# Gated linear attention: exponentials written in their layout of use, score copies and square sums on ScalarE

## The chip, the cores and the metric

The kernel runs on one core of one Trainium2 chip. The metric is the time of one execution on the device in microseconds (us); each kernel is run several times and the median counts. The engines are called PE (TensorE, matmuls), DVE (VectorE), ACT (ScalarE), POOL (GpSimd) and SP (SyncE, which here issues the loads and stores).

## The reference

The program is one layer of a bidirectional encoder for two sequences (called samples 0 and 1) of 512 tokens with 1024 features: a SwiGLU block, a mixing block, a second SwiGLU block and a gated input embedding. The mixing block has attention heads and four heads of gated linear attention (GLA) side by side. The change touches GLA alone. Per head (64 features of q and k, 128 of v) and per chunk of 64 tokens the reference computes

```python
cum = jnp.cumsum(log_a.reshape(bsz, nc, c, h, dk), axis=2)
mid = cum[:, :, c // 2 - 1:c // 2]
last = cum[:, :, c - 1:]
scores = jnp.einsum('bnihd,bnjhd->bnhij', q * jnp.exp(cum - mid), k * jnp.exp(mid - cum))
scores = jnp.where(mask, scores, 0.0)
o_intra = jnp.einsum('bnhij,bnjhe->bnihe', scores, v)
upd = jnp.einsum('bnjhd,bnjhe->bnhde', k * jnp.exp(last - cum), v)
...
o_inter = jnp.einsum('bnihd,bnhde->bnihe', q * jnp.exp(cum), states)
```

once forward (a token sees itself) and once backward (it does not). `states` is the running sum of `upd`, decayed from chunk to chunk. The two directions are added, each head's 128 values are divided by their root mean square, and the result is multiplied with a gate.

## The kernel before

The program has four stages: the first SwiGLU block, the mixing block, the second SwiGLU block and the end. PE's order is written out by hand: generators yield after each small piece of work, and a main generator of large matmuls is woven with a side generator by counts (the table PLAN). For DVE, ACT, POOL and SP a scheduler orders the instructions that the code issues, and each engine then works through its own list strictly in that order. Buffers come from pools: a pool of four PSUM banks (`bank_d`, named pd in the profile) serves all matmuls of GLA, another (pm) the large ones. `m8` is a pool of three large SBUF buffers, which take in turn the decays, the exponentials E, the decayed q and k (z, whose tile is named qk1; the profile calls it qk) and the states W; `m2` is one of six smaller buffers. A tile that takes over a buffer waits until the last reader of the old content is done.

GLA runs at the end of the mixing block, woven with the output projection's matmuls (L716, three per yield, in two or more yields between the pieces). Heads go in pairs; there are two pairs per sample, so four pairs, called first to fourth. `gla(s)` yields four generators for a sample:

- `pre(hp)` prepares a pair. Loads on SP bring the log decays l (L985, 4 issues) and q and k (L987, 2 issues) into one tile lq, with the two heads one above the other in the 128 partitions, 64 each. Four groups of matmuls (L999, two directions by two halves of the tokens) make the sums of the decays. Behind each, ACT writes exp(+) and exp(-) into E (the helper's line, L177), and DVE copies small columns sc (L1003), which become ex (L1010, L1012) and, through ACT, the chunk decays R. L1017 multiplies q and k with E into z: in z a head has 128 partitions, the forward direction in the lower 64 and the backward one in the upper 64, so each piece is a 64-partition product that moves from one half to the other; eight of them per pair.
- `one(h)` does a head: transposes of k (L1031) into a bank, copied by ACT to kT (L1033); the update matmuls (L1038) into two banks U; the chain of states: two copies by ACT (L1045, L1046), then six steps per direction on DVE (L1048, L1050), each reading a part of U and the state before it; POOL then scales all states with R (L1051, L1052). Score matmuls (L1060) fill two banks, S[0] forward and S[1] backward, and L1062 copies from each the entries under a mask into A, on DVE.
- `two_a(h)` makes the head's output in a bank: A times v (L1071) plus q times W (L1074). L1077 squares it on ACT into osq, L1079 sums the squares on DVE, the rms steps follow, and L1082 multiplies bank, rms and gate into G.
- `two_b(h)` transposes G (L1089) and splits it into a high and a low part (L1090 ACT, L1091 DVE) for the output projection.

Per pair PE does `one` for the even and the odd head, `two_a` for both, then `pre` of the next pair with its four groups, then `two_b` for both. Weights are loaded (raw), and split into a high part by ACT (L138) and a low part by POOL or DVE (L139).

Of the kernel before, what the change touches and what calls it, by code (L numbers as in the profile page):

```python
# [12 lines left out]
AF = mybir.ActivationFunctionType  # L13
ALU = mybir.AluOpType
AX = mybir.AxisListType
# [5 lines left out]
NT = 4  # L21
# [14 lines left out]
            A=(157, 159, 160),  # L36
            seg=((2, 132), (2, 142), (18, 160), (18, 170), (43, 193), (43, 216), (178, 334)),
            b=(4, 3),
# [685 lines left out]
class Middle:  # L724
# [246 lines left out]
    def gla(self, s):  # L971
        nc, L = self.nc, self.L
        f, bw = slice(0, 64), slice(64, 128)
        T = {}

        def pre(hp):
            if hp == 0:
                T["mx"] = L.xp.tile([128, 4, 2, 512], F32R, tag="x", name="mixG")
                self.mix[s, 0] = T["mx"]
                T["A"] = self.vp.tile([128, 2, NT, 128], F32, tag="v", name="A")  # L980
                nc.gpsimd.memset(T["A"], 0.0)
            lq = self.m8("lq", (128, 2, 2, 512))
            l, qk = lq[:, 0].rearrange("p d (t c) -> p d t c", t=NT), lq[:, 1]
            for t in range(NT):
                nc.sync.dma_start(l[:, :, t], self.spill["l", s][t].rearrange("p (d c) -> p d c", d=2)[:, :, hp * 128:(hp + 1) * 128])  # L985
            for i in range(2):
                nc.sync.dma_start(qk[:, i], self.spill["gqk", s][2 * i + hp])  # L987
            yield
            R = [self.sp.tile([128, 8], F32, tag=f"R{e}", name=f"R{e}", bufs=2) for e in range(2)]
            E = self.m8("E", (128, 2, 2, 512))  # L990
            z = self.m8("qk1", (128, 2, 2, 512))
            for e in range(2):
                T["z", 2 * hp + e], T["R", 2 * hp + e] = z[:, e], R[e]
            for dr in range(2):
                sc = self.sp.tile([128, 2, 8], F32, tag="sc", name="sc")
                for hf in range(2):
                    b = L.bank_d().rearrange("p (a n) -> p a n", a=2)
                    for a in range(2):
                        nc.tensor.matmul(b[:, a, :132], l[:, dr, 2 * hf + a], self.L.U[:, dr], start=True, stop=True)  # L999
                    for j, sg in ((0, 1.0), (1, -1.0)):  # L1000
                        L.expln(E[:, dr, j, hf * 256:(hf + 1) * 256].rearrange("p (a n) -> p a n", a=2),
                                             b[:, :, :128], AF.Exp, scale=sg)
                    nc.vector.tensor_copy(  # L1003
                        sc[:, :, hf * 4:hf * 4 + 4].rearrange("p k (a c) -> p a k c", a=2),
                        b[:, :, 128:132].rearrange("p a (k c) -> p a k c", k=2))
                    if hf == 0:
                        yield
                ex = self.sp.tile([128, 7], F32, tag="ex", name="ex")
                if dr == 0:
                    nc.vector.tensor_tensor(ex, sc[:, 1, 0:7], sc[:, 0, 1:8], ALU.add)  # L1010
                else:
                    nc.vector.tensor_tensor(ex, sc[:, 1, 1:8], sc[:, 0, 0:7], ALU.add)  # L1012
                for e in range(2):
                    rs, rd = slice(64 * e, 64 * e + 64), slice(64 * dr, 64 * dr + 64)
                    L.expln(R[e][rd, 1 - dr:8 - dr], ex[rs], AF.Exp)
                    for i in range(2):
                        nc.vector.tensor_tensor(z[rd, e, i], qk[rs, i], E[rs, dr, i], ALU.mult)  # L1017
                yield

        def one(h):  # L1020
# [8 lines left out]
            b = L.bank_d()  # L1029
# [26 lines left out]
            for t in range(NT):  # L1056
                ts = slice(t * 128, (t + 1) * 128)
                for dr in range(2):
                    rd = slice(64 * dr, 64 * dr + 64)
                    nc.tensor.matmul(S[dr][:, t], k1[rd, ts], q1[rd, ts], start=True, stop=True)  # L1060
            for dr in range(2):
                nc.vector.copy_predicated(A, self.L.mask[:, dr].unsqueeze(1).to_broadcast([128, NT, 128]), S[dr])  # L1062
            T["h", h] = gv, G, W, A
            yield

        def two_a(h):
            gv, G, W, A = T["h", h]
            q1 = T["z", h][:, 0]
            o = L.bank_d().rearrange("p (a n) -> p a n", a=4)
            for t in range(NT):  # L1070
                nc.tensor.matmul(o[:, t], A[:, t], gv[:, t], start=True, stop=False)  # L1071
                for cc in range(2):
                    c = 2 * t + cc
                    nc.tensor.matmul(o[64 * cc:64 * cc + 64, t], q1[:, c * 64:(c + 1) * 64], W[:, c],  # L1074
                                     start=False, stop=True)
            sq = self.m2("osq", shape=(128, NT, 128))
            nc.scalar.activation(sq, o, AF.Square)  # L1077
            ss = L.small(NT, "oss")
            nc.vector.tensor_reduce(ss, sq, AX.X, ALU.add)  # L1079
            r = self.rms(ss, NT, 128.0, GN_EPS, "gn")  # L1080
            for t in range(NT):
                nc.vector.scalar_tensor_tensor(G[:, t], o[:, t], r[:, t:t + 1], G[:, t], ALU.mult, ALU.mult)  # L1082
            yield
# [365 lines left out]
```

## Time and profile before

| what | value |
|---|---|
| time, median of 3 runs | 1935.41 us (1934.36 to 1936.28) |
| the profiled execution: its time | 1935.19 us |
| the profiled execution: its span | 1933.4 us |
| mean granted clock of PE | 0.992 |
| PE busy | 1867.3 us, 97% of the span |
| DVE busy | 1406.2 us, 73% |
| ACT busy | 874.0 us, 45% |
| POOL busy | 822.3 us, 43% |

The span runs from the first to the last instruction. An engine's busy time counts its instructions alone. In a row of a timeline stand start, duration, engine, line, operation, what is written and read, the shapes and the count, and in brackets the idle time before it with the instruction that ended the idle time. GLA lies between about 985 and 1130 us of the span.

### The profile page before, as it was taken

How to read it: one execution, taken by the hardware profiler on the slowest of the kernel's cores; microseconds unless marked ns; L12 is line 12 of the kernel's file. 1: busy time of each engine (PE TensorE's matmuls, PEld its weight loads, DVE VectorE, ACT ScalarE, POOL GpSimd, SP SyncE). 2: the span in 40 equal slices, each digit the busy share in tenths (PEclk: the TensorE clock that was granted, in tenths of full speed). 3: DMA queues.
4: the chain of work that ended last, by engine and by line, in shares of the span. 5: the costliest groups of instructions: out<-in, count | busy, mean ns of one | idle time of the engine just before them, and what ended most of it. 6: DMA issues, size and time to landing. Idle time of an engine off the chain costs nothing. (4 is left out here: it accounts for less than half of the span.)

```text
span 1933.4 us, 25273 instructions
## 1 busy us (share of the span) xinstructions
PE 1867.3 (97%) x8838; PEld 1529.5 (79%) x8838; DVE 1406.2 (73%) x2173; ACT 874.0 (45%) x1654; POOL 822.3 (43%) x614
## 2 busy tenths in 40 slices
PE   7999999999999998989999898999999999999999
PEld 5788888888888887777876577888888888888787
DVE  7856566657786985788778878656566568995973
ACT  6444544544231355657743356445444442231442
POOL 0665566552450023432234444654665561451243
PEclk9999999999999999999999998999999999999999
DMA  4434443468876233222443332335444388766242
GB/s 181 152 115 153 174 158 142 166 261 336 307 271 231 75 133 123 77 87 91 144 148 88 99 109 89 141 114 185 159 153 153 142 308 335 300 247 235 77 131 77
DMA packets 104959, 322.22 MB, mean 167 GB/s; under 512 B 11008, under 2 KB 38400, under 8 KB 99456
## 3 DMA queue, kind: packets, MB, share of 16 engines
q1 hardware_dynamic: 101376, 314.32, 45.3%
q10 hardware_dynamic: 3456, 6.29, 0.9%
q8 instruction: 70, 1.15, 0.3%
q14 instruction: 57, 0.47, 0.1%
HBM read 218.85 MB, written 101.71 MB: 166 GB/s over the span
## 5 line engine op out<-in xcount | busy, mean ns | idle before, releaser
L139 POOL TENSOR_TENSOR w<-raw,w 128x512 fp32r<-128x512 f32 (+1 forms) x288 | 391.5, 1367 | 651.6 <-ACT w L138 602.0
L138 ACT ACTIVATE w<-raw 128x512 fp32r<-128x512 f32 (+1 forms) x586 | 363.0, 624 | 435.2 <-POOL raw L270 85.2
L270 POOL TENSOR_TENSOR raw<-raw 128x512 f32<-128x512 f32 x240 | 356.8, 1494 | 226.2 <-DVE w L139 159.0
L426 PE MATMUL pm<-X,w 128*128 128x512 f32 x1848 | 435.2, 393 | 10.5 <-ACT X L138 7.4
L426 PEld LDWEIGHTS pm<-X,w 128*128 128x128 f32 x1848 | 348.1, 189 | 89.0 <-ACT X L138 8.2
L139 DVE TENSOR_TENSOR w<-raw,w 128x512 fp32r<-128x512 f32 (+1 forms) x298 | 281.9, 954 | 117.2 <-ACT w L138 113.2
L426 PE MATMUL pd<-X,w 128*128 128x512 f32 x1320 | 309.2, 392 | 2.9 <-DVE w L139 2.2
L426 PEld LDWEIGHTS pd<-X,w 128*128 128x128 f32 x1320 | 248.6, 189 | 57.9 <-DVE w L139 3.0
L540 PE MATMUL pm<-w,XB 128*128 128x512 f32 x864 | 198.4, 390 | 0.8 <-DVE Y L524 0.8
L540 PEld LDWEIGHTS pm<-w,XB 128*128 128x128 f32 x864 | 162.0, 188 | 35.2 <-DVE Y L524 1.6
L139 DVE TENSOR_TENSOR hs<-sg,hs 128x512 fp32r<-128x512 f32 (+1 forms) x182 | 145.2, 817 | 49.5 <-ACT hs L138 48.4
L716 PE MATMUL pm<-w,h1T 128*128 128x512 f32 (+1 forms) x768 | 180.2, 377 | 0.0
L138 ACT ACTIVATE hs<-sg 128x512 fp32r<-128x512 f32 (+1 forms) x182 | 98.4, 561 | 165.1 <-DVE sg L392 64.3
L716 PEld LDWEIGHTS pm<-w,h1T 128*128 128x128 f32 x768 | 133.1, 191 | 20.7
L540 PE MATMUL pd<-w,XB 128*128 128x512 f32 x648 | 148.8, 389 | 0.0
L540 PEld LDWEIGHTS pd<-w,XB 128*128 128x128 f32 x648 | 121.7, 188 | 25.2
L524 DVE TENSOR_TENSOR Y<-Y,pm 128x512 f32<-128x512 f32 x104 | 70.5, 683 | 35.4 <-PE pm L540 35.4
L372 DVE TENSOR_TENSOR sg<-u,pm 128x512 f32<-128x512 f32 x22 | 15.1, 687 | 108.9 <-PE pm L426 108.9
L716 PE MATMUL pm<-w,h3T 128*128 128x512 f32 x384 | 90.6, 393 | 0.0
L716 PEld LDWEIGHTS pm<-w,h3T 128*128 128x128 f32 x384 | 71.3, 188 | 14.7 <-DVE h3T L671 0.2
L661 ACT ACTIVATE pd<-pd,c_lnT 128x512 f32<-128x512 f32 x48 | 36.0, 751 | 92.8 <-PE pd L659 92.8
L524 DVE TENSOR_TENSOR Y<-Y,pd 128x512 f32<-128x512 f32 x88 | 58.7, 679 | 17.6 <-PE pd L540 17.6
(237 smaller groups left out, 2512.8 us busy)
## 6 DMA issues: line engine op xcount, KB each, us to landing
hs<-hs SPq DMA_DIRECT2D x126, 512.0 KB, 2.6
XB<-hs SPq DMA_DIRECT2D x42, 1536.0 KB, 6.8
raw<-in_wgu SPq DMA_DIRECT2D x88, 512.0 KB, 3.4
raw<-in_wd SPq DMA_DIRECT2D x36, 512.0 KB, 7.1
hs_t<-hs SPq DMA_DIRECT2D x56, 256.0 KB, 2.4
XB<-hs_t SPq DMA_DIRECT2D x26, 512.0 KB, 4.9
raw<-in_wout SPq DMA_DIRECT2D x16, 512.0 KB, 3.6
raw<-in_wpg SPq DMA_DIRECT2D x16, 512.0 KB, 3.6
```

The costliest lines, as they stand in the source:

```text
L138: first = nc.scalar.activation(hi, raw, AF.Copy)
L139: (eng or nc.vector).tensor_tensor(lo, raw, hi.bitcast(F32), ALU.subtract)
L270: (sums or self.nc.gpsimd).tensor_tensor(o(), x(), y(), ALU.subtract)
L372: add = lambda o, x, y: nc.vector.tensor_tensor(o, x, y, ALU.add)
L426: nc.tensor.matmul(bank, w[:, a, kt * 128:(kt + 1) * 128], X[k][:, kt, b], start=(k in (0, 1, 4) and kt == 0 and m == 0), stop=(kt == 3 an ...
L524: nc.vector.tensor_tensor(yv, yv, bank, ALU.add)
L540: nc.tensor.matmul(b[t], h[:, a, t * 128:(t + 1) * 128], d[:, c], start=(k in (0, 4, 1) and g == 0 and x == 0), stop=(g == len(H) - 1 and ...
L661: nc.scalar.activation(p, p, AF.Identity, scale=self.lnT[:, c:c + 1], bias=self.lnT[:, c + 8:c + 9])
L716: nc.tensor.matmul(banks[t][:, :width], x[:, i, t * 128:(t + 1) * 128], w[a][:, j], start=(q == 0 and a == 0 and m == 0), stop=(q == nq - ...
```

## The change

All line numbers of the kernel after are one to three higher than before in this stretch. The change has four parts.

1. l gets an m8 tile of its own. q and k are loaded straight into z, twice, once into the lower and once into the upper 64 partitions (L992, four issues instead of two).
2. E is written in z's layout: each exponential of 128x256 becomes two of 64x256, one per head, which write to the direction's 64 partitions. One in-place multiplication of 128x1024 per head (L1019), behind the second direction, takes the place of four of 64x512.
3. ACT copies the diagonal 64x64 blocks of S[1] to A (L1064, two copies of 64x4x64 per head); one predicated copy (L1065) then writes the forward entries from S[0] over them.
4. The square on ACT is made per token tile with an accumulated sum (L1082, four instructions of 128x128), and the reduction on DVE goes.

```diff
@@ -979,16 +979,17 @@
                 self.mix[s, 0] = T["mx"]
                 T["A"] = self.vp.tile([128, 2, NT, 128], F32, tag="v", name="A")
                 nc.gpsimd.memset(T["A"], 0.0)
-            lq = self.m8("lq", (128, 2, 2, 512))
-            l, qk = lq[:, 0].rearrange("p d (t c) -> p d t c", t=NT), lq[:, 1]
+            l = self.m8("l", (128, 2, 2, 512))[:, 0].rearrange("p d (t c) -> p d t c", t=NT)
             for t in range(NT):
                 nc.sync.dma_start(l[:, :, t], self.spill["l", s][t].rearrange("p (d c) -> p d c", d=2)[:, :, hp * 128:(hp + 1) * 128])
-            for i in range(2):
-                nc.sync.dma_start(qk[:, i], self.spill["gqk", s][2 * i + hp])
             yield
             R = [self.sp.tile([128, 8], F32, tag=f"R{e}", name=f"R{e}", bufs=2) for e in range(2)]
             E = self.m8("E", (128, 2, 2, 512))
             z = self.m8("qk1", (128, 2, 2, 512))
+            for i in range(2):
+                src = self.spill["gqk", s][2 * i + hp].rearrange("(e p) c -> p e c", e=2)
+                for rd in (f, bw):
+                    nc.sync.dma_start(z[rd, :, i], src)
             for e in range(2):
                 T["z", 2 * hp + e], T["R", 2 * hp + e] = z[:, e], R[e]
             for dr in range(2):
@@ -997,9 +998,10 @@
                     b = L.bank_d().rearrange("p (a n) -> p a n", a=2)
                     for a in range(2):
                         nc.tensor.matmul(b[:, a, :132], l[:, dr, 2 * hf + a], self.L.U[:, dr], start=True, stop=True)
-                    for j, sg in ((0, 1.0), (1, -1.0)):
-                        L.expln(E[:, dr, j, hf * 256:(hf + 1) * 256].rearrange("p (a n) -> p a n", a=2),
-                                             b[:, :, :128], AF.Exp, scale=sg)
+                    for e in range(2):
+                        for j, sg in ((0, 1.0), (1, -1.0)):
+                            L.expln(E[64 * dr:64 * dr + 64, e, j, hf * 256:(hf + 1) * 256].rearrange("p (a n) -> p a n", a=2),
+                                    b[64 * e:64 * e + 64, :, :128], AF.Exp, scale=sg)
                     nc.vector.tensor_copy(
                         sc[:, :, hf * 4:hf * 4 + 4].rearrange("p k (a c) -> p a k c", a=2),
                         b[:, :, 128:132].rearrange("p a (k c) -> p a k c", k=2))
@@ -1013,8 +1015,8 @@
                 for e in range(2):
                     rs, rd = slice(64 * e, 64 * e + 64), slice(64 * dr, 64 * dr + 64)
                     L.expln(R[e][rd, 1 - dr:8 - dr], ex[rs], AF.Exp)
-                    for i in range(2):
-                        nc.vector.tensor_tensor(z[rd, e, i], qk[rs, i], E[rs, dr, i], ALU.mult)
+                    if dr == 1:
+                        nc.vector.tensor_tensor(z[:, e], z[:, e], E[:, e], ALU.mult)
                 yield
 
         def one(h):
@@ -1058,8 +1060,9 @@
                 for dr in range(2):
                     rd = slice(64 * dr, 64 * dr + 64)
                     nc.tensor.matmul(S[dr][:, t], k1[rd, ts], q1[rd, ts], start=True, stop=True)
-            for dr in range(2):
-                nc.vector.copy_predicated(A, self.L.mask[:, dr].unsqueeze(1).to_broadcast([128, NT, 128]), S[dr])
+            for r in (f, bw):
+                nc.scalar.activation(A[r, :, r], S[1][r, :, r], AF.Copy)
+            nc.vector.copy_predicated(A, self.L.mask[:, 0].unsqueeze(1).to_broadcast([128, NT, 128]), S[0])
             T["h", h] = gv, G, W, A
             yield
 
@@ -1074,9 +1077,9 @@
                     nc.tensor.matmul(o[64 * cc:64 * cc + 64, t], q1[:, c * 64:(c + 1) * 64], W[:, c],
                                      start=False, stop=True)
             sq = self.m2("osq", shape=(128, NT, 128))
-            nc.scalar.activation(sq, o, AF.Square)
             ss = L.small(NT, "oss")
-            nc.vector.tensor_reduce(ss, sq, AX.X, ALU.add)
+            for t in range(NT):
+                nc.scalar.activation(sq[:, t], o[:, t], AF.Square, accum_out=ss[:, t:t + 1])
             r = self.rms(ss, NT, 128.0, GN_EPS, "gn")
             for t in range(NT):
                 nc.vector.scalar_tensor_tensor(G[:, t], o[:, t], r[:, t:t + 1], G[:, t], ALU.mult, ALU.mult)
```

The change also moves instructions. First PE, in the third pair, from the end of the even head's scores over the odd head's transposes to its update matmuls (pd and a number is one PSUM bank's tile, qk1 is z, w and mixA belong to the output projection; the brackets name the engines or load queues whose semaphores are waited for). Before:

```order
L1060 MATMUL pd_9481<-qk1_9333 128x128
L716 MATMUL pm_9271<-w_9103,mixA_6014 128x512 x3
L1031 MATMUL pd_9505<-c_ident_3477,qk1_9333 128x128 [waits DVE_49,Activation_49]
L1031 MATMUL pd_9505<-c_ident_3477,qk1_9333 128x128 x3
L716 MATMUL pm_9271<-w_9106,mixA_6014 128x512 x3
L1038 MATMUL pd_9516<-gvh_9495,kT_9510 128x128 [waits DMAHW4_49,DVE_49,Activation_49]
L1038 MATMUL pd_9517<-gvh_9495,kT_9510 128x128 [waits PE_49]
```

and of the kernel after:

```order
L1062 MATMUL pd_9505<-qk1_9351 128x128
L716 MATMUL pm_9289<-w_9117,mixA_6014 128x512 x3
L1033 MATMUL pd_9530<-c_ident_3477,qk1_9351 128x128 [waits PE_49,Activation_49]
L1033 MATMUL pd_9530<-c_ident_3477,qk1_9351 128x128 x3
L716 MATMUL pm_9289<-w_9120,mixA_6014 128x512 x3
L1040 MATMUL pd_9541<-gvh_9520,kT_9535 128x128 [waits DMAHW0_49,DVE_49,Activation_49]
L1040 MATMUL pd_9542<-gvh_9520,kT_9535 128x128 [waits DVE_49]
```

The sequence is the same, but the odd head's transposes no longer wait for DVE: their bank is now one that ACT and PE release. Both update banks now wait for DVE.

Next PE at the even head's output in the same pair, behind the odd head's scores. Before:

```order
L1060 MATMUL pd_9560<-qk1_9333 128x128
L716 MATMUL pm_9544<-w_9275,mixG_8603 128x512
L716 MATMUL pm_9544<-w_9275,mixG_8603 128x512 [waits Pool_49]
L716 MATMUL pm_9544<-w_9275,mixG_8603 128x512
L716 MATMUL pm_9545<-w_9272,mixG_8603 128x512 x3
L1071 MATMUL pd_9577<-gvh_9423,A_9318 128x128 [waits DVE_49,Activation_49]
L1074 MATMUL pd_9577<-W_9454,qk1_9333 64x128 [waits Pool_49]
```

and of the kernel after:

```order
L1062 MATMUL pd_9585<-qk1_9351 128x128
L716 MATMUL pm_9569<-w_9293,mixG_8603 128x512
L716 MATMUL pm_9569<-w_9293,mixG_8603 128x512 [waits Pool_49]
L716 MATMUL pm_9569<-w_9293,mixG_8603 128x512
L716 MATMUL pm_9570<-w_9290,mixG_8603 128x512 x3
L1074 MATMUL pd_9603<-gvh_9447,A_9338 128x128 [waits PE_49,Activation_49]
L1077 MATMUL pd_9603<-W_9478,qk1_9351 64x128 [waits Pool_49]
```

The first output matmul waits for PE and ACT instead of DVE and ACT; the wait for POOL, which scales W, is as before.

Then ACT between the odd head's output of the second pair and kT of the third pair's two heads (osq: squares; gna, gny: rms steps; E, R: exponentials). Before:

```order
L177 ACTIVATE R_9331<-ex 64x7
L177 ACTIVATE E<-pd 128x256 x2
L138 ACTIVATE w<-raw 128x512
L1090 ACTIVATE mixG<-pd,c_gn 128x512
L177 ACTIVATE R_9330<-ex 64x7
L177 ACTIVATE R_9331<-ex 64x7
L1090 ACTIVATE mixG<-pd,c_gn 128x512
L1033 ACTIVATE kT<-pd 128x512
L1045 ACTIVATE W<-pd 64x128
L1046 ACTIVATE W<-pd 64x128
L138 ACTIVATE w<-raw 128x512
L1033 ACTIVATE kT<-pd 128x512
```

and of the kernel after:

```order
L177 ACTIVATE E<-pd 64x256 x6
L138 ACTIVATE w<-raw 128x512
L177 ACTIVATE R_9348<-ex 64x7
L177 ACTIVATE R_9349<-ex 64x7
L138 ACTIVATE w<-raw 128x512
L1093 ACTIVATE mixG<-pd,c_gn 128x512 x2
L1035 ACTIVATE kT<-pd 128x512
L1047 ACTIVATE W<-pd 64x128
L1048 ACTIVATE W<-pd 64x128
L1064 ACTIVATE A<-pd 64x4x64 x2
L138 ACTIVATE w<-raw 128x512
L1035 ACTIVATE kT<-pd 128x512
```

The weight splits (L138) of this stretch stand behind all exponentials now, the second R pair is ahead of both mixG, and the even head's two copies to A, like the split behind them, stand between its W copies and the odd head's kT.

On SP the four loads of q and k for the second to fourth pair now wait for PE (the last reader of the buffer that z takes over), stand behind a weight load, and have the next pair's v and gate loads behind them; before, the two loads followed those of l and waited for a queue slot alone.

## The prediction

> **What bounds the kernel now.** I read the page first, then PE's waits over the stretch that the diff touches, then each engine's timeline there.
>
> ```profile
> PE 1867.3 (97%) x8838; PEld 1529.5 (79%) x8838; DVE 1406.2 (73%) x2173; ACT 874.0 (45%) x1654; POOL 822.3 (43%) x614
> ```
>
> TensorE (PE) is busy for 1867.3 of 1933.4 us, and the change takes no matmul away. What can be won is PE's idle time, and only where the gated linear attention (GLA) runs, about 985 to 1130 us. PE's waits there, with total, count and longest:
>
> ```profile
> PE pd L1031 <- DVE W L1048: 7.5, 4, 3.1
> PE pd L1031 <- DVE qk L1017: 5.5, 4, 1.8
> PE pd L1071 <- DVE W L1048: 5.0, 4, 1.3
> PE pd L1089 <- DVE Gh L1082: 0.8, 1, 0.8
> ```
>
> There are four head pairs, and each has three waits, all on VectorE (DVE): before the even head's transposes for the decayed q and k (5.5 us in all), before the odd head's transposes (7.5) and before the even head's output (5.0) for the state chain. The sum with the last line, 18.8 us, is the ceiling of any gain from waits. The busy time per stretch (PE, PEld, DVE, ACT, POOL, then PE's granted clock) shows who is full:
>
> ```profile
> 1100.00:1110.00 10.00, 6.81 (x54) 5.10 (x55) 9.60 (x21) 2.50 (x6) 4.17 (x7) 1.00 0.22 65
> 1110.00:1120.00 10.00, 8.94 (x62) 6.17 (x60) 7.68 (x18) 1.05 (x3) 4.66 (x4) 0.83 0.01 2
> ```
>
> Where PE drops to 6.81 of 10 us, DVE has 9.60 and ScalarE (ACT) 2.50. In the next stretch PE's clock is 0.83. So work moved from DVE to ACT can pay here. How much is seen in one head pair, the third, on PE (start, duration, idle before):
>
> ```profile
> 1066.06 0.63 PE L1031 MATMUL pd<-c_ident,qk 128*128 128x128 f32 x4 [1.05 <-DVE qk L1017]
> ...
> 1071.85 0.96 PE L716 MATMUL pm<-w,mixA 128*128 128x512 f32 x3
> 1074.05 0.63 PE L1031 MATMUL pd<-c_ident,qk 128*128 128x128 f32 x4 [1.24 <-DVE W L1048]
> ...
> 1075.37 1.16 PE L1038 MATMUL pd<-gvh,kT 64*128 64x128 f32 x16
> ...
> 1077.36 1.16 PE L1060 MATMUL pd<-qk 64*128 64x128 f32 x16
> 1078.45 1.66 PE L716 MATMUL pm<-w,mixG 128*128 128x512 f32 x6
> 1081.43 0.46 PE L1071 MATMUL pd<-gvh,A 128*128 128x128 f32 x2 [1.32 <-DVE W L1048]
> ...
> 1085.67 0.44 PE L1074 MATMUL pd<-W,qk 128*64 128x128 f32 x4
> ...
> 1088.40 1.65 PE L716 MATMUL pm<-w,mixG 128*128 128x512 f32 x6
> ```
>
> and on DVE (the last link of the even chain) and POOL (GpSimd, the second scaling of the odd states):
>
> ```profile
> 1073.94 0.35 DVE L1050 SCALAR_TENSOR_TENSOR W<-W,R,pd 64x128 f32<-64x128 f32 x1
> ```
> ```profile
> 1083.18 1.68 POOL L1052 TENSOR_TENSOR W<-W,R 64x896 f32<-64x896 f32 x1
> ```
>
> The odd transposes have their input long before; they wait for a PSUM bank that the even chain still reads.
>
> **Bank release (copies of A on ACT).** ACT now reads the second score bank right after the score matmuls, and in the order of the changed kernel the odd transposes and the even output wait for ACT, no longer for DVE. Work it through for this pair. The odd transposes can start when L716 ends, 1072.81, 1.24 earlier; kT is then copied by about 1074.15 (transposes to matmuls now take 1075.37 - 1074.05 = 1.32). What is late next is the update matmuls' own two banks, which the chain frees at 1073.94 + 0.35 = 1074.29. L1038 starts at 1074.32, 1.05 earlier than 1075.37. The odd scores come at 1076.31, L716 behind them ends at 1079.06, and the even output needs a bank freed by ACT's two copies after 1077.47: two of 64x256 size at 0.38 (row below), ready by 1078.3, no wait. That is 2.4 us earlier than 1081.43. But the odd output needs W after both scalings on POOL, and the odd chain moves only with L1038, by 1.05. Now POOL ends at 1083.18 + 1.68 = 1084.86 and PE reads W at 1085.67, so there are 0.81 us of slack. The pair's output thus ends 1.05 + 0.81 = 1.86 earlier, with a new wait of about half a us on POOL. The other pairs have the same waits and matmuls; I take 1.8 for each, **7.2 us** for four. If POOL or a late copy takes more, only the slack is left (0.8 each, 3.2); if POOL were no bound, 2.4 each, 9.6.
>
> **Exponentials in the layout of use, one multiplication per head.** The groups by shape (busy, mean ns of one, idle before):
>
> ```profile
> L1017 DVE TENSOR_TENSOR qk<-lq,E 64x512 f32<-64x512 f32 x32 | 25.1, 806 | 0.4
> ...
> L1062 DVE COPY_PREDICATED A<-c_mask,pd 128x512 f32<-128x512 uint32 x16 | 11.6, 727 | 0.4
> ...
> L177 ACT ACTIVATE E<-pd 128x256 f32<-128x256 f32 x32 | 10.7, 375 | 5.9 <-PE pd L999 5.9
> ...
> L1079 DVE TENSOR_REDUCE oss<-osq 128x4 f32<-128x512 f32 x8 | 5.5, 685 | 8.4 <-ACT osq L1077 8.4
> ...
> L1077 ACT ACTIVATE osq<-pd 128x512 f32<-128x512 f32 x8 | 4.8, 598 | 33.4 <-PE pd L1074 33.4
> ...
> L943 ACT ACTIVATE o<-pd 64x256 f32<-64x256 f32 x2 | 0.8, 376 | 1.5 <-PE pd L940 1.5
> ```
>
> A multiplication of 128x1024 has this row from another stage:
>
> ```profile
> L652 DVE TENSOR_TENSOR Y<-Y,lnr 128x1024 f32<-128x1024 f32 x8 | 9.7, 1218 | 0.0
> ```
>
> DVE loses 32 x 0.806 = 25.1 and gets 8 x 1.22 = 9.7; half of the predicated copies go (5.8) and all reductions (5.5): some 27 us less on DVE. The even transposes wait only for the even head's product. Before, three or four 64-partition pieces stand in their way behind the last exponential, now one piece of 1.22. ACT's exponentials become 64 of 64x256. Half the partitions cost the same (376 against 375 ns), so 32 are added; but two in a row take 0.64, not 0.75:
>
> ```profile
> 1092.52 0.64 ACT L177 ACTIVATE E<-pd 128x256 f32<-128x256 f32 x2
> ```
>
> so each added one costs 0.64 - 0.375 = 0.27, 8.5 us in all, and 0.54 for each of four steps in a pair. The last one then ends about half a us later. On ACT, the third pair's last exponentials and the even kT:
>
> ```profile
> 1061.84 0.63 ACT L177 ACTIVATE E<-pd 128x256 f32<-128x256 f32 x2
> ...
> 1066.73 0.60 ACT L1033 ACTIVATE kT<-pd 128x512 f32<-128x512 f32 x1 [0.36 <-PE pd L1031]
> ```
>
> They were over at 1062.5, 3.5 us ahead of the transposes, and DVE's queue no longer stands between. The ceiling is the 5.5 us of wait: 1.05 in the third pair, 1.78 in the fourth (below), 2.7 in the first two. I take 0.6 of the third's, since POOL may be in the way, 1.4 of the fourth's, 0.7 for the second. The first pair has no pair ahead to hide its loads and exponentials, and its R exponentials now stand ahead of kT on ACT: -0.4, between -0.7 and +0.4. Sum **2.3 us**, bounds -1 and 5.5.
>
> The rows on POOL and DVE at that place in the third pair:
>
> ```profile
> 1061.70 3.48 POOL L139 TENSOR_TENSOR w<-raw,w 128x512 fp32r<-128x512 f32 x2 [8.71 <-ACT w L138]
> ```
> ```profile
> 1064.06 1.14 DVE L1012 TENSOR_TENSOR ex<-sc 128x7 f32<-128x7 f32 x1
> ```
>
> The sum of 128x7, ahead of the products, took 1.14 us and ended at 1065.20, with the POOL pair (1065.18). This speaks against the change: a large product can lose most of a POOL split (3.48 / 2 = 1.7). [...]
>
> **Loads.** q and k now go straight into z, twice, in four loads for two, and z's buffer is free only when the pair before has read it. SP's queue and the loads' landing:
>
> ```profile
> 1037.72 1.08 SPq L987 DMA_DIRECT2D lq<-sp_gqk  x2
> ```
> ```profile
> lq<-sp_gqk SPq DMA_DIRECT2D x8, 256.0 KB, 4.1
> ```
>
> PE's first row behind the last read, ahead of the third pair:
>
> ```profile
> 1055.13 1.65 PE L716 MATMUL pm<-w,mixA 128*128 128x512 f32 x6
> ```
>
> Four issues of 0.54 and 4.1 to land are 6.3 us after that read: 1061.4. The exponentials last until 1062.5 now and 1063 then: hidden by 1.6 us. If twice the bytes take twice as long, 4 us are added, and z is 2.5 late: the 2.3 us are lost, as in the POOL case. The v and gate loads queue behind on SP by at most these 6.3 - 4.1 = 2.2 us; they are needed at L1038, 12 us after that read. I cost this at nothing.
>
> **Square sums on ACT.** Four instructions of 128x128 take the place of one of 0.598 and a DVE reduction of 0.685. The nearest rows with an accumulator:
>
> ```profile
> 984.98 0.68 ACT L177 ACTIVATE P<-pd,nm 128x512 f32<-128x512 f32 x1
> 985.55 0.20 ACT L177 ACTIVATION_READ_ACCUMULATOR P<-pd,nm 128x1 f32 x1
> 985.64 0.64 ACT L138 ACTIVATE w<-raw 128x512 fp32r<-128x512 f32 x1
> ```
>
> Behind such a pair the next instruction starts 0.66 after the first's start (985.64 - 984.98). Four quarter-size ones cost between 4 x 0.2 = 0.8 and 4 x 0.66 = 2.6; with the read's 0.1 and a body of some 0.25, I take 1.4 (an estimate from these rows), beside 1.28 before: nothing on the path. [...] The wait of 0.8 at L1089 stays.
>
> **Clock.** The fourth pair has the longest wait:
>
> ```profile
> 1100.08 0.63 PE L1031 MATMUL pd<-c_ident,qk 128*128 128x128 f32 x4 [1.78 <-DVE qk L1017]
> ...
> 1109.24 0.63 PE L1031 MATMUL pd<-c_ident,qk 128*128 128x128 f32 x4 [3.11 <-DVE W L1048]
> ...
> 1110.83 2.08 PE L1038 MATMUL pd<-gvh,kT 64*128 64x128 f32 x16
> ```
>
> After 3.11 us idle, L1038 takes 2.08 in place of 1.16, and the odd chain waits for it. The wait of 1.24 in the third pair is followed by 1.16 for the same line: no dip. With the transposes out of that wait, less than 2 us stay in one piece: **0.9 us** more.
>
> **The sum.** 7.2 + 2.3 + 0.9 = 10.4. I take 0.9 off for ACT's order: weight splits (L138, 0.64 each) now stand among kT, the copies and the W copies in the third and fourth pair. That leaves 9.5. The profiled execution took 1935.19 (span 1933.4 and 1.8 around it), 0.2 under the median of 1935.41. Forecast: 1935.2 - 9.5 = 1925.7, with the 0.2 **1926**. The least by the low ends is 3.2 from slack and nothing else, 1932; the most 9.6 + 3.7 + 0.9 = 14.2, 1921.
>
> **Rivals.**
> *Bank release moves the wait only.* The copies on ACT come late (behind weight splits), and the even chain or POOL gates the same matmuls. Then only the 2.3 and a part of the clock stay: about 2.6, 1932.6. For it: L1038 still needs the chain's banks. Against: ACT has 2.5 us of work in the 10 where PE is idle most.
> *The large products wait for POOL, or for their loads.* The 2.3 us become -2.5 (four POOL splits of 1.2 more): 9.5 - 4.8 = 4.7, 1930.5. For it, the 1.14 row; against, one product replaces four pieces.
> *ACT becomes the bound: slower.* Between the odd output and the even kT, ACT's queue now holds 4 squares, 16 exponentials, 4 R, 2 rms steps, 2 mixG and 2 splits. At full durations, 2.6 + 16 x 0.376 + 6 x 0.2 + 2 x 0.69 + 2 x 0.64 = 12.5 us (0.2 and 0.69 estimated from the read and the 128x512 rows); the trace has 1066.7 - 1055.1 = 11.6 there. With in-order waits it decides as soon as less than 0.09 of overlap per instruction is had: 1.2 in each of three transitions and 0.7 in the first pair, and copies behind it free no bank earlier: +4.3, 1939.5. Against: the overlap of two exponentials is in the trace.
>
> **Chances.** Forecast 0.63, POOL or loads 0.11, wait moved only 0.17, ACT bound 0.09. A measurement of this kernel can tell about 0.2%, 3.9 us, from no change. Of the forecast 0.61 lies beyond that, of the POOL case 0.09: faster 0.7; the rest of both and the moved wait, same 0.21; slower 0.09. The range runs from 1921 to 1933: all but the slower case and a part beyond its ends.
>
> **What would show it.** In the changed profile: no wait of the odd transposes on the state chain (7.5 before) and none of the even output (5.0); a wait of L1077 on POOL of about 0.5 per pair; the clock at 1.00 in the fourth pair; DVE about 27 us less, ACT about 20 more (8.5, 16 copies of 0.376, and 0.8 for each head's squares). Wrong if L1040, the update matmuls of the changed kernel, or the even transposes take these waits over, if ACT is named as releaser of L1033 or L1040, or if z's loads are.

## The result and the profile after

| | before | after |
|---|---|---|
| median | 1934.88 us (6 runs, 1933.06 to 1944.01) | 1924.83 us (6 runs, 1922.94 to 1927.06) |
| span of the profiled execution | 1933.4 us | 1924.0 us |

The ratio is 0.9939 with an interval of 0.9922 to 0.9955: the changed kernel is 10 us faster, against 9.5 forecast, and its 1924.83 lies within the forecast range of 1921 to 1933. The single runs of one kernel differ with PE's mean granted clock (the kernel before, on one chip, from 1932.5 us at 0.992 to 1946.1 at 0.986), which will matter below.

The page's first line after the change:

```profile
PE 1868.5 (97%) x8838; PEld 1530.5 (80%) x8838; DVE 1383.0 (72%) x2133; ACT 896.1 (47%) x1758; POOL 825.5 (43%) x614
```

PE does the same work. DVE has 1406.2 - 1383.0 = 23 us less (27 forecast), ACT 22 more (20 forecast). PE's waits in the GLA stage (total, count, longest; two of 0.2 us are left out):

```profile
PE pd L1040 <- ACT kT L1035: 3.8, 4, 2.1
PE pd L1077 <- POOL W L1054: 3.2, 4, 1.1
PE pd L1033 <- ACT mixG L1093: 0.9, 1, 0.9
PE pd L1040 <- ACT w L138: 0.8, 1, 0.8
PE pd L1092 <- DVE Gh L1085: 0.6, 1, 0.6
PE pd L1033 <- ACT w L138: 0.4, 1, 0.4
```

The three waits on DVE that made up 18.0 us (7.5, 5.5 and 5.0) are gone. What came in their place is 3.2 us on POOL (0.8 per pair, about 0.5 forecast) and 5.9 us on ACT (3.8, 0.9, 0.8, 0.4). That ACT is named as releaser of L1033 and L1040 is one of the things that the prediction had called a sign of being wrong. The third pair on PE, to be laid beside the rows of the prediction:

```profile
1062.11 0.63 PE L1033 MATMUL pd<-c_ident,qk 128*128 128x128 f32 x4 [0.35 <-ACT w L138]
...
1068.61 0.66 PE L1033 MATMUL pd<-c_ident,qk 128*128 128x128 f32 x4
...
1070.77 1.49 PE L1040 MATMUL pd<-gvh,kT 64*128 64x128 f32 x16 [0.80 <-ACT w L138]
...
1075.68 0.38 PE L1074 MATMUL pd<-gvh,A 128*128 128x128 f32 x2
...
1080.64 0.44 PE L1077 MATMUL pd<-W,qk 128*64 128x128 f32 x4 [0.73 <-POOL W L1054]
```

The odd transposes (1068.61) and the even output (1075.68) have no idle time before them; the odd output waits 0.73 for POOL. The stage as a whole runs from the first sums of decays (L999, then L1000) to the last transposes of G (L1089, then L1092). Before:

```profile
988.46 0.65 PE L999 MATMUL pd<-c_U,lq 128*128 128x132 f32 x4
...
1130.38 1.01 PE L1089 MATMUL pd<-c_ident,Gh 128*128 128x128 f32 x4 [0.75 <-DVE Gh L1082]
```

and after:

```profile
989.10 0.70 PE L1000 MATMUL pd<-c_U,l 128*128 128x132 f32 x4
...
1120.51 1.10 PE L1092 MATMUL pd<-c_ident,Gh 128*128 128x128 f32 x4 [0.59 <-DVE Gh L1085]
```

From first start to last start it took 141.9 us before and takes 131.4 after: 10.5 us, about the whole of what the span lost (9.4) and more. This stage length leaves out what differs in the rest of the program. It can be compared only with an eye on the clock: a ten-us slice with the clock at 0.83 stands for some 1.7 us, (1 - 0.83) x 10, as an estimate. The stage before holds one such slice (the prediction shows it), the stage after none.

### The profile page after: what moved, and what is told of

The parts are those of the page before. It is cut to its first block, busy times and chain, and to the rows that moved or that the text cites. A ratio compares the mean times of both kernels' runs of the same rounds, so it can differ in the third digit from the quotient of the medians.

```text
span 1924.0 us, 25319 instructions
## 1 busy us (share of the span) xinstructions
PE 1868.5 (97%) x8838; PEld 1530.5 (80%) x8838; DVE 1383.0 (72%) x2133; ACT 896.1 (47%) x1758; POOL 825.5 (43%) x614
## 5 line engine op out<-in xcount | busy, mean ns | idle before, releaser
L138 ACT ACTIVATE w<-raw 128x512 fp32r<-128x512 f32 (+1 forms) x586 | 363.6, 625 | 432.4 <-POOL raw L270 87.1
L426 PE MATMUL pm<-X,w 128*128 128x512 f32 x1848 | 435.3, 393 | 11.5 <-ACT X L138 8.6
L138 ACT ACTIVATE hs<-sg 128x512 fp32r<-128x512 f32 (+1 forms) x182 | 98.6, 563 | 165.0 <-DVE sg L392 64.1
L524 DVE TENSOR_TENSOR Y<-Y,pd 128x512 f32<-128x512 f32 x88 | 58.8, 679 | 17.6 <-PE pd L540 17.6
```

The costliest lines, as they stand in the source:

```text
L138: first = nc.scalar.activation(hi, raw, AF.Copy)
L426: nc.tensor.matmul(bank, w[:, a, kt * 128:(kt + 1) * 128], X[k][:, kt, b], start=(k in (0, 1, 4) and kt == 0 and m == 0), stop=(kt == 3 an ...
L524: nc.vector.tensor_tensor(yv, yv, bank, ALU.add)
```

## The experiments

Every kernel ran in five rounds beside the kernel before; four kernels at a time share a chip. The table gives the medians, the median of the kernel before on that chip, the ratio with its interval, and from the profile the stage length and the sum of PE's waits in the stage (for the kernel before 19.0: the prediction's 18.8 and one wait of 0.2 that it left out).

| kernel | median | before there | ratio | stage | PE waits |
|---|---|---|---|---|---|
| kernel before, its own profile | | | | 141.9 | 19.0 |
| copies on ACT alone (`a1_copies`) | 1926.96 | 1938.22 | 0.9938 (0.9918 to 0.9957) | 133.7 | 11.5 |
| layout alone (`a2_layout`) | 1938.43 | 1938.22 | 0.9999 (0.9980 to 1.0018) | 145.1 | 16.3 |
| squares alone (`a3_squares`) | 1937.45 | 1938.22 | 0.9995 (0.9980 to 1.0011) | 147.8 | 17.9 |
| copies, predicated copy twice (`a4_copies_twice`) | 1929.23 | 1938.22 | 0.9946 (0.9925 to 0.9967) | 135.6 | 10.1 |
| changed kernel again (`c0_after`) | 1926.16 | 1935.93 | 0.9947 (0.9927 to 0.9968) | 131.5 | 10.0 |
| its copies on DVE (`b1_dve_copies`) | 1933.93 | 1935.93 | 0.9987 (0.9966 to 1.0009) | 140.3 | 17.6 |
| changed, sc first (`b2_sc_first`) | 1921.44 | 1935.93 | 0.9924 (0.9905 to 0.9944) | 129.1 | 7.7 |
| changed, half of the scaling on DVE (`b3_half_dve`) | 1933.71 | 1935.93 | 0.9981 (0.9967 to 0.9994) | 140.0 | 13.9 |
| copies alone again (`d1_copies`) | 1926.59 | 1937.97 | 0.9938 (0.9927 to 0.9950) | 133.8 | 10.3 |
| copies alone, sc first (`d2_copies_sc`) | 1928.41 | 1937.97 | 0.9952 (0.9938 to 0.9966) | 134.1 | 10.8 |
| changed, sc first again (`d3_sc_first`) | 1921.20 | 1937.97 | 0.9916 (0.9902 to 0.9930) | 130.3 | 7.7 |
| as before it, without the squares (`d4_sc_no_squares`) | 1920.56 | 1937.97 | 0.9911 (0.9898 to 0.9924) | 128.6 | 7.3 |

### The four parts one by one

`a1_copies` is the kernel before with this edit alone:

```diff
-            for dr in range(2):
-                nc.vector.copy_predicated(A, self.L.mask[:, dr].unsqueeze(1).to_broadcast([128, NT, 128]), S[dr])
+            for r in (f, bw):
+                nc.scalar.activation(A[r, :, r], S[1][r, :, r], AF.Copy)
+            nc.vector.copy_predicated(A, self.L.mask[:, 0].unsqueeze(1).to_broadcast([128, NT, 128]), S[0])
```

> The kernel before with the third part alone: ScalarE copies the diagonal blocks of the second score bank to A, one predicated copy follows. Theory (the early release of that bank is what pays): the waits of the odd transposes (7.5 us) and of the even output (5.0) on the state chain go, a wait of about 0.5 us per pair on GpSimd comes, the wait for the decayed q and k (5.5) stays, the clock dip in the fourth pair goes: 7 to 8 us less than before. Rival (the gain goes with the work taken from VectorE, 27 us for 9.9 us won): 5.8 us of VectorE work go, so about 2 us less.

Its waits of PE:

```profile
PE pd L1031 <- DVE qk L1017: 5.7, 4, 1.8
PE pd L1075 <- POOL W L1052: 3.2, 4, 1.1
PE pd L1038 <- DVE W L1048: 1.2, 1, 1.2
```

As the theory had it: the 12.5 us of waits of the odd transposes and the even output on the chain are gone, POOL's 3.2 came, and the 5.7 for q and k stayed. New are 1.2 us at the fourth pair's update matmuls, whose banks the chain frees. The stage is 8.2 us shorter; the forecast had 7.2 for the banks and 0.9 for the clock. It fits pair by pair: counted from the stage's start, the four pairs bring the end of the odd output forward by 2.0, 1.7, 1.5 and 3.0 us (1.9, 1.7, 1.5 and 2.9 in `d1_copies`, the same kernel on another chip), where 1.8 each was forecast and 0.9 more in the fourth. The medians say 11 us, more than the 7 to 8 expected. In the executions of the two kernels on this chip whose mean clock is 0.992 or 0.993 (five of each) the medians are 1934.3 and 1926.8, 7.5 apart; the other four us go with the clock (below).

`a2_layout` has the new loads, the split exponentials and the products of 128x1024, with copies and squares as before:

```diff
-            lq = self.m8("lq", (128, 2, 2, 512))
+            l = self.m8("l", (128, 2, 2, 512))[:, 0].rearrange("p d (t c) -> p d t c", t=NT)
...
-                    for i in range(2):
-                        nc.vector.tensor_tensor(z[rd, e, i], qk[rs, i], E[rs, dr, i], ALU.mult)
+                    if dr == 1:
+                        nc.vector.tensor_tensor(z[:, e], z[:, e], E[:, e], ALU.mult)
```

> The kernel before with the first two parts alone: loads straight into z, exponentials in z's layout, one multiplication per head. Theory: the wait for the decayed q and k shrinks from 5.5 us, the two waits on the state chain stay near 12.5 together: 2 to 3 us less than before. Rival (gain by VectorE work): 15 us of VectorE work go, so 5 to 6 us less.

```profile
PE pd L1033 <- DVE W L1050: 7.1, 4, 2.2
PE pd L1073 <- DVE W L1050: 4.9, 4, 1.3
PE pd L1040 <- ACT kT L1035: 3.0, 3, 2.1
PE pd L1033 <- ACT mixG L1092: 0.9, 2, 0.5
```

The chain's waits are all there (12.0), the wait for q and k (5.5) is gone, and ACT takes 4.3 of it back (3.0, 0.9 and 0.4 more): 2.7 us less waiting in all (19.0 to 16.3). The total time does not show that (ratio 0.9999, 2 to 3 us less expected), and the rival's 5 to 6 us are not there either. Nine of its twelve executions ran at a mean clock of 0.988 or 0.989, of the kernel before five of 23. The stage of this profile holds a stretch with a low clock (the eighth column):

```profile
1080.00:1090.00 10.00, 8.67 (x44) 5.48 (x42) 5.93 (x17) 1.01 (x3) 4.35 (x3) 0.71 0.16 52
1090.00:1100.00 10.00, 10.00 (x42) 7.46 (x39) 3.03 (x12) 3.61 (x11) 0.90 (x1) 0.61 0.53 131
```

It takes some 7 us, (0.29 + 0.39) x 10, without which the stage would be about 138.

`a3_squares` has the accumulated squares alone:

```diff
-            nc.scalar.activation(sq, o, AF.Square)
             ss = L.small(NT, "oss")
-            nc.vector.tensor_reduce(ss, sq, AX.X, ALU.add)
+            for t in range(NT):
+                nc.scalar.activation(sq[:, t], o[:, t], AF.Square, accum_out=ss[:, t:t + 1])
```

> The kernel before with the fourth part alone: four squares with accumulated sums in place of one square and a reduction. Theory: nothing (within 0.5 us), since the rms chain is covered by the matmuls between the output and its transposes. Rival (gain by VectorE work): 5.5 us of it go, about 2 us less.

It gives nothing that can be measured: a ratio of 0.9995, its ends 4 us below and 2 above. (Its profile's stage of 147.8 holds ten-us slices with the clock at 0.95, 0.84, 0.50 and 0.85, some 8 us; the 141.9 of the kernel before hold one at 0.83.) `a4_copies_twice` is the first of these with the remaining predicated copy written twice, so that DVE has its work of before again (DVE busy 1404.6 us against 1406.2):

```diff
+            nc.vector.copy_predicated(A, self.L.mask[:, 0].unsqueeze(1).to_broadcast([128, NT, 128]), S[0])
             nc.vector.copy_predicated(A, self.L.mask[:, 0].unsqueeze(1).to_broadcast([128, NT, 128]), S[0])
```

> As the run with the third part alone, but the remaining predicated copy is issued twice, so that VectorE does as much as before and only the release of the bank differs. Theory: 6.5 to 8 us less than before, at most 0.5 short of the run without the second copy. Rival (gain by VectorE work): no gain.

DVE's work is back and the gain stays at 9 us. It is 2.3 short of the copies alone where at most 0.5 was expected; the ranges of the runs overlap (1925.2 to 1931.0, 1926.1 to 1928.9), and the profile's stage of 135.6 holds one ten-us slice with the clock at 0.83, or 1.7 us, without which it would be 133.9, close to the 133.7 of the copies alone. By the theory of work taken from DVE there would be no gain here; it falls.

### The bank, from the other side

`b1_dve_copies` is the changed kernel with one word changed, the diagonal copies now behind the chain on DVE:

```diff
-                nc.scalar.activation(A[r, :, r], S[1][r, :, r], AF.Copy)
+                nc.vector.tensor_copy(A[r, :, r], S[1][r, :, r])
```

> The changed kernel itself, to stand beside the three runs below on one chip and beside the kernel with the copies alone (11 us under the kernel before on its chip, of which about 4 are a clock that is lower in the runs of the kernel before). Theory: the copies bring nearly all, the layout 1 to 2 us on top, the squares nothing: 10 to 13 us less than before. Rival (the layout eats on ScalarE what it saves on VectorE): the same 11 us as with the copies alone.

> The changed kernel with the two diagonal copies per head on VectorE instead of ScalarE; all else stays, and ScalarE is relieved of 6 us. Theory (the release of the bank is what pays): the copies stand behind the state chain on VectorE, the waits of the odd transposes and the even output on the chain come back at 12 us together, and the time is within 3 us of the kernel before. Rival (relief of VectorE as a whole): VectorE still has 20 us less than before, so most of the gain stays, 7 us or more.

```profile
PE pd L1033 <- DVE W L1050: 7.1, 4, 2.2
PE pd L1074 <- DVE W L1050: 5.3, 4, 1.3
PE pd L1040 <- ACT kT L1035: 3.0, 3, 2.1
```

The waits on the chain are back at 12.4 us and the stage at 140.3, though DVE has 20 us less to do than before and ACT is relieved. The time is within the noise of the kernel before. With `a4_copies_twice` this shows what pays: that the bank's release does not stand behind the chain in DVE's queue, and not how much work is taken from DVE. No run had DVE copy the bank ahead of the chain, so the engine and the place in its queue are not told apart. The changed kernel itself gave 9.8 us on this chip, just short of the 10 to 13 expected and of the rival's 11. Its stage is 2.3 us shorter than with the copies alone (131.4 and 131.5 against 133.7 and 133.8, two profiles each). The total time does not show this difference: beside the kernel before on the same chip, the ratio is 0.9938 twice for the copies alone, and 0.9939 and 0.9947 for the changed kernel.

### What is late next

After the change DVE's longest wait in the stage is a new one. Before, and in the changed kernel:

```profile
DVE sc L1003 <- ACT E L177: 1.9, 2, 1.3
```
```profile
DVE sc L1005 <- ACT E L177: 11.0, 10, 2.1
```

sc reads eight columns of the bank from which the exponentials read, and waits until they are done: four now in place of two, and each takes 0.37 us. ex and R hang on sc, and R stands ahead of kT in ACT's queue. In the first pair of the changed kernel, on ACT and on DVE:

```profile
1001.28 0.43 ACT L177 ACTIVATE R<-ex 64x7 f32<-64x7 f32 x2 [1.79 <-DVE ex L1014]
1001.74 0.60 ACT L1035 ACTIVATE kT<-pd 128x512 f32<-128x512 f32 x1
```
```profile
995.30 0.17 DVE L1012 TENSOR_TENSOR ex<-sc 128x7 f32<-128x7 f32 x1
...
998.89 1.22 DVE L1019 TENSOR_TENSOR qk<-qk,E 128x1024 f32<-128x1024 f32 x1
1000.02 1.23 DVE L1014 TENSOR_TENSOR ex<-sc 128x7 f32<-128x7 f32 x1
```

and on POOL:

```profile
999.12 3.33 POOL L139 TENSOR_TENSOR w<-raw,w 128x512 fp32r<-128x512 f32 x2 [3.25 <-ACT w L138]
```

ACT sat idle for 1.79 us, most of it with kT's input ready (the transposes ended at 999.6), and PE waited 2.07 for kT. Two things made the second ex late: it came behind both products, and, while POOL's weight split ran, it took 1.23 us where the first ex had taken 0.17. `b2_sc_first` puts the small read first, which brings ex ahead of the products as well (in the first pair the second two R start 9.5 us after the stage does, in place of 12.2):

```diff
+                    nc.vector.tensor_copy(
+                        sc[:, :, hf * 4:hf * 4 + 4].rearrange("p k (a c) -> p a k c", a=2),
+                        b[:, :, 128:132].rearrange("p a (k c) -> p a k c", k=2))
                     for e in range(2):
...
-                    nc.vector.tensor_copy(
-                        sc[:, :, hf * 4:hf * 4 + 4].rearrange("p k (a c) -> p a k c", a=2),
-                        b[:, :, 128:132].rearrange("p a (k c) -> p a k c", k=2))
```

> The changed kernel with the small copy sc issued ahead of the four exponentials that read the same bank, so that it does not wait behind them (11.0 us of waits on VectorE in the changed kernel), and ex and R come earlier. Theory: the waits of the update matmuls and transposes on ScalarE (5.9 us in four pairs, of which 2.1 in the first pair, where kT stands behind R) shrink to 2 to 4: 2 to 3 us less than the changed kernel. Rival: ScalarE's queue is bound by its own work, the waits stay, and the time is the changed kernel's within 1 us.

```profile
PE pd L1077 <- POOL W L1054: 2.8, 4, 0.8
PE pd L1040 <- ACT kT L1035: 2.6, 3, 1.3
PE pd L1033 <- PE pm L716: 1.4, 2, 1.0
```

The waits on ACT fall from 5.7 (in `c0_after`) to 2.6, and the median by 4.7 us where 2 to 3 were expected (1926.16 to 1921.44; the ranges of the runs, 1924.7 to 1927.5 and 1919.7 to 1925.0, hardly touch). PE's waits fell by 2.3 and the stage by 2.4 (by 1.2 in `d3_sc_first`, whose stage holds a slice with the clock at 0.83). The spans of these two profiles differ by 4.2: beside the stage's 2.4, 0.7 lie ahead of it and 1.1 behind it, outside GLA. The new order has its price too. In the second pair sc stands on DVE behind rms steps and multiplications of G (L188, L1085), and ACT's exponentials wait for it:

```profile
1023.76 1.31 ACT L177 ACTIVATE E<-pd 64x256 f32<-64x256 f32 x4 [2.07 <-DVE sc L1001]
```

PE's wait for kT in this pair grew from 0.39 to 1.30 us; the first, third and fourth pair win 1.8, 0.9 and 1.0, the second loses 1.2.

`b3_half_dve` goes for the other new wait, on POOL:

```diff
-            nc.gpsimd.tensor_tensor(W[bw, 0:7], W[bw, 0:7], R[bw, 0:7].unsqueeze(2).to_broadcast([64, 7, 128]), ALU.mult)
+            nc.vector.tensor_tensor(W[bw, 0:7], W[bw, 0:7], R[bw, 0:7].unsqueeze(2).to_broadcast([64, 7, 128]), ALU.mult)
```

> The changed kernel with the backward half of the state scaling on VectorE, the forward half stays on GpSimd. Theory: the odd output's wait on GpSimd (3.2 us in four pairs) was the next to come and goes: 2 to 3 us less than the changed kernel. Rival: VectorE's half stands ahead of the predicated copy, or the two halves hinder each other at SBUF, and the wait moves to the copy A or to the longer halves: within 1 us of the changed kernel or slower.

It is 7.5 us slower than the changed kernel (1933.71 to 1926.16), where 2 to 3 less were expected. Some of its waits, and DVE and POOL in the third pair:

```profile
PE pd L1062 <- DVE A L1065: 4.1, 3, 1.9
PE pd L1077 <- DVE W L1054: 1.6, 2, 1.1
PE pd L1074 <- DVE A L1065: 1.5, 1, 1.5
```
```profile
1078.18 2.87 DVE L1054 TENSOR_TENSOR W<-W,R 64x896 f32<-64x896 f32 x1
1081.08 0.72 DVE L1065 COPY_PREDICATED A<-c_mask,pd 128x512 f32<-128x512 uint32 x1
```
```profile
1077.18 1.68 POOL L1053 TENSOR_TENSOR W<-W,R 64x896 f32<-64x896 f32 x1 [5.56 <-DVE W L1050]
1078.83 3.35 POOL L139 TENSOR_TENSOR w<-raw,w 128x512 fp32r<-128x512 f32 x2
```

The rival holds, above all in its first form: DVE's half stands ahead of the predicated copy that frees the first score bank (4.1 us of new waits for it at L1062, 1.5 at L1074). The second form shows in one of the eight: beside POOL's instructions it took 2.87 us where the median is 1.59 (that they meet at SBUF no run shows). PE's waits are 3.9 us more and the stage 8.5 longer; 3.4 of the difference is a slice with the clock at 0.66.

### Does the layout pay at all?

Three kernels beside the copies alone, on one chip: the copies with sc first in the layout before, the changed kernel with sc first, and that without the squares (their edits are those above).

> The kernel with the copies alone once more, to stand beside the three runs below on one chip. Theory: by PE's idle time in the profiles (11.5 us with the copies alone, 10.1 in the changed kernel, 7.7 in the changed kernel with sc first) it is 3 to 5 us over the changed kernel with sc first, and about 10 under the kernel before.

> The copies alone, and sc ahead of the exponentials, in the layout before. Theory (the layout pays only where ex and R are not late): the wait of the even transposes for the eight 64-partition products stays near 5.5 us, so within 1.5 us of the copies alone and 2 to 4 us over the changed kernel with sc first. Rival (the layout brings nothing, sc first everything): as the changed kernel with sc first, within 1 us.

> The changed kernel with sc first once more, as the measure for the others: 13 to 15 us under the kernel before.

> The changed kernel with sc first, but with the square and the reduction of the kernel before. Theory: the squares bring nothing, within 1 us of the run with them. Rival: 5.5 us more on VectorE between the outputs and the next pair's products cost 1.5 us or more.

With sc first the layout, squares included, is worth 7.2 us (1928.41 to 1921.20), more than the 2 to 4 expected. The changed kernel with sc first is 16.8 under the kernel before (13 to 15 expected), and the copies alone are 5.4 over it (3 to 5 expected). In the layout before, sc first brings nothing (1928.41 beside 1926.59, with overlapping ranges): its wait of PE for the products stays:

```profile
PE pd L1031 <- DVE qk L1017: 6.1, 4, 1.9
PE pd L1075 <- POOL W L1052: 3.2, 4, 1.1
```

So the two edits need each other: with one product per head in place of four the wait for the products goes (6.1 us here, 0.3 in `d3_sc_first`), and the early sc takes R out of kT's way on ACT. Of the 7.2 the stage shows 3.8 (134.1 to 130.3) and the waits 3.1. The spans of the two profiles differ by 7.4; 2.1 of this lie ahead of the stage, where the slices with a lowered clock add up to 10.2 us in one and 8.5 in the other, and 1.5 behind it. So about half of the 7.2 is seen in GLA, and the rest is not shown to come from the edit. The squares are worth nothing in this company either (1921.20 with, 1920.56 without). The fastest kernel of the study is that one, 1920.56 us, ratio 0.9911 to the kernel before; with the squares kept it is 0.9916.

## Why the prediction was right

**Bank release, 7.2 us:** right, in mechanism and size. The copies alone shorten the stage by 8.2, forecast with the clock term 8.1, and by pairs as forecast (above); PE's waits fall by 7.5 to 8.7. The odd transposes and the even output start without a wait, and POOL's scaling of W is what the odd output waits for, with 0.8 us per pair where about 0.5 was forecast.

**Layout, 2.3 us, less 0.9 for ACT's order:** the 2.3 us of stage between the copies alone and the changed kernel, squares included, stand beside 1.4 forecast for both terms; the total time does not show them. Pair by pair they are -0.8, 1.1, 0.2 and 1.8, with -0.4, 0.7, 0.6 and 1.4 forecast ahead of the 0.9. How they come about was not as told. I expected POOL to stand in the way of the products and kept back 2.8 of the 5.5 us of wait. One of the eight products did take 2305 ns (least, median and most in the row below), but the wait for the products vanished entirely:

```profile
L1019 DVE TENSOR_TENSOR qk<-qk,E x8: 1217/1226/2305, 997.7 to 1094.0; 128x1024 f32<-128x1024 f32 x8
```

On the other side ACT was charged with 1.3 (0.4 in the first pair and the 0.9), and its waits are 5.9. That these two errors go against each other and leave a sum near the forecast is luck.

The step that failed is the 1.3 us for ACT: it counted the work on ACT, not what ACT waits for. Of the 5.7 us of waits on ACT in `c0_after`, 3.1 go when sc is read first, so they hang on sc, ex and R, which the prediction did not follow; the other 2.6 stay.

**Clock, 0.9 us:** the dip of the profile is gone in both profiles of the changed kernel (the clock from 990 to 1120 is 1.00 in `c0_after`). The slice with the fourth pair's odd transposes and its update matmuls, after:

```profile
1100.00:1110.00 10.00, 9.21 (x74) 6.44 (x72) 9.17 (x24) 2.13 (x6) 4.54 (x3) 1.00 0.31 107
```
```profile
1102.42 1.16 PE L1040 MATMUL pd<-gvh,kT 64*128 64x128 f32 x16 [0.79 <-ACT kT L1035]
```

1.16 in place of 2.08. The reason given, that less than 2 us of idle time stay in one piece, does not hold. `d1_copies` has the dip after 1.79 us, where `a1_copies`, the same kernel, took 1.16 after 1.78:

```profile
1093.15 0.63 PE L1031 MATMUL pd<-c_ident,qk 128*128 128x128 f32 x4 [1.79 <-DVE qk L1017]
...
1094.47 1.92 PE L1038 MATMUL pd<-gvh,kT 64*128 64x128 f32 x16
```

So that the dip is missing in one profile is in part luck, and the clock is worth more than one execution shows, see below.

**Loads and squares, nothing:** right. z's loads land in 4.7 us each (4.1 before, with half as many), in the third pair issued at 1051.97 to 1054.5 and used at 1060.67. In the first pair DVE waits 0.5 us for a load ahead of the first product; PE does not wait for it. Four squares with their reads follow each other every 0.25 us, 1.1 in all (1.4 estimated):

```profile
1051.98 0.28 ACT L1082 ACTIVATE osq<-pd 128x128 f32<-128x128 f32 x1 [2.40 <-PE pd L1077]
...
1052.25 0.27 ACT L1082 ACTIVATE osq<-pd 128x128 f32<-128x128 f32 x1
```

**ACT's order, 0.9 us off:** the place was right (a split ahead of kT costs 0.80 in the third pair, see above), and the size too small by far, as said under the layout. By pairs, the end of the odd output came earlier by 1.2, 2.7, 1.8 and 4.7 us (1.4, 2.5, 2.4 and 4.1 forecast, ahead of the 0.9 for ACT in the third and fourth), taken from the stage's start.

**The rivals.** The wait did move, to POOL and ACT, but not the whole of it. ACT holds PE in every pair: 2.07 us in the first, where R's wait held kT, and 0.4 to 0.9 at a time in the others. The kernel is not slower for it, as it would have been by the third rival.

Two slips in the working change nothing in the forecast time. 32 x 0.806 is 25.8; the 25.1 is the row's busy time. The upper end of the gain has 3.7 for the layout where the text's bound is 5.5; with 5.5 the range would have begun at 1919.

## What to carry to other kernels

When PE waits for a PSUM bank, ask which engine reads it last and what that engine has queued in front: a second engine that copies the bank out early can be worth more than the work taken off the busy one (here 9.0 us with DVE's work as before, in `a4_copies_twice`, and 2.0, within the noise, with 20 us less of it, in `b1_dve_copies`). When two engines read one bank, try the short read first if others hang on it; here it paid 4.7 us in the new layout and brought nothing in the old one (1928.41 beside 1926.59). Where each run differs with the clock, compare beside the total the length of the stage that the edit touches, in the profiles, and look for slices with a lowered clock in it.

## What the runs showed of the clock

The kernel before, in its 23 runs on one chip, took from 1932.5 us at a mean granted clock of 0.992 to 1946.1 at 0.986; the changed kernel and the copies alone stayed within 1923 to 1929 at 0.992 to 0.994. The prediction took the clock to fall only after an idle time near 3 us, from one row with 3.11. In the layout alone, after two shorter ones:

```profile
1074.96 0.63 PE L1033 MATMUL pd<-c_ident,qk 128*128 128x128 f32 x4 [2.22 <-DVE W L1050]
...
1082.35 0.46 PE L1073 MATMUL pd<-gvh,A 128*128 128x128 f32 x2 [1.33 <-DVE W L1050]
...
1083.52 0.44 PE L1076 MATMUL pd<-W,qk 128*64 128x128 f32 x4
...
1084.36 0.70 PE L1076 MATMUL pd<-W,qk 128*64 128x128 f32 x4
```

the same four matmuls go from 0.44 to 0.70 us, and the clock stays low for some 14 us. The same four go from 0.44 to 0.70 for some 7 us after one wait of 1.49 us in `b3_half_dve`. In the kernel before, idle times of 1.1 to 1.8 us left the clock alone in the profiled execution. So in some executions the clock is lowered behind waits of 1.3 to 2.2 us, and in others it is not. What decides it is not shown. That fewer waits make the clock steadier is what the spreads of these kernels suggest, but the changed kernel with sc first, which has the fewest waits of these, spread again in `d3_sc_first`, from 1919.4 to 1925.9 at 0.990 to 0.995. No run set the waits and the clock apart.
